# Strassen's sums of weights in the w2 stages: two made by VectorE, two by adding transfers, and five folds in place of six

## The chip, the cores and the metric

The kernel runs on one core of a Trainium2 chip. The metric is the device time of one execution in microseconds (us); lower is better. The core's engines work side by side and wait for one another by semaphores: TensorE (PE: matmuls; PEld is its loading of the stationary operand), VectorE (DVE), ScalarE (ACT), GpSimd (POOL) and SyncE (SP), whose queue here mostly issues transfers. A transfer is issued from an engine's queue and carried out by the core's DMA engines.

## The reference

A decoder trunk of two layers over 256 tokens of width 1024, in float32. Each layer has two half-step feed-forward blocks with a mixer of two branches between them, each followed by a layer norm:

```python
def _swiglu(x, w1, w3, w2):
    return (jax.nn.silu(x @ w1) * (x @ w3)) @ w2

for l in range(DEPTH):                                   # DEPTH = 2
    h = _swiglu(x, ffn_w1[l, 0], ffn_w3[l, 0], ffn_w2[l, 0])
    x = _layernorm(ALPHA * x + 0.5 * h, ln_g[l, 0], ln_b[l, 0])
    h = _mixer(x, l, ...)
    x = _layernorm(ALPHA * x + h, ln_g[l, 1], ln_b[l, 1])
    h = _swiglu(x, ffn_w1[l, 1], ffn_w3[l, 1], ffn_w2[l, 1])
    x = _layernorm(ALPHA * x + 0.5 * h, ln_g[l, 2], ln_b[l, 2])
```

The change concerns the last product of `_swiglu`, with w2: (256 x 2816) times (2816 x 1024). It occurs four times, two layers by two feed-forward blocks; each occurrence is called a w2 stage here.

## The kernel before, in words

Every matmul runs on operands split in two: `hi`, a rounded copy that ScalarE makes, and `lo`, what is left, which VectorE makes by a subtraction (`split`, lines 225 and 227; in `stream`, lines 183 and 185). A product of float32 matrices is then three matmuls: hi by hi, lo by hi, hi by lo. Weights come from HBM in pieces of 128 x 2048 float32 (1 MB). `fetch` (transfer at line 161, on SP's queue) takes a buffer from `raw_pool`, which has four; a buffer is free again when both halves of its piece have been split (or used in a sum). Half a piece, 128 x 1024, is the unit of the splits. The hi and lo pools have eight tiles each.

The hidden activations are in 22 blocks of 128 (k = 0 to 21), the 256 tokens in two blocks (t = 0, 1), the 1024 output columns in two halves (c = 0, 1). `gemm_seven` is a w2 stage. The blocks k = 0 to 7 (a 2 x 2 arrangement of tokens by hidden blocks, times the pieces w11, w12, w21, w22 of four k blocks by one column half) go by Strassen's scheme in Winograd's form: seven products (`product`, line 355, 12 matmuls each) in place of eight. The left sides of four of them are sums of activations, `sums[0]` to `sums[3]`, made beforehand. The right sides of four are sums of weights, of which three build on one another in the buffer r1: w11 + w12, then + w22, then + w21; the fourth is w12 + w22. `gather` (lines 336 to 340) makes such a sum by two adding transfers of 512 KB each, issued from GpSimd's queue (line 339), which add the second piece from HBM onto the buffer.

The products accumulate in PSUM banks, two of them side banks, `bx` and `bz`. Where a product belongs to more than one output block, `ln.fold` (line 567) lets VectorE add or subtract the side bank onto the token tile `xtok`, at 128 x 512. The remaining hidden blocks, k = 8 to 21, are ordinary matmuls (`rows`, line 370). Those of column half 0 are cut into seven pieces of 12 matmuls and stand between the products (`between`), those of column half 1 follow in the end (`held`). Their weights come in the fetches of k = 8, 12, 16 and 20, called R8, R12, R16 and R20 here, one set for each column half.

TensorE's order is the program's; the instructions of the other engines are put in order by a scheduler from priorities that `step()` moves on with each fetch or gather, and from an estimate of when their operands are there. Each engine works through its own queue in that order. Besides the weights the stage has, on the queues of the others: the last two hidden blocks, whose transposes go as transfers on SP's queue (line 202) with copies on GpSimd before and after (lines 198 and 207); the loads of the norm's gain and bias (line 534, GpSimd's queue), in the last stage with a scaling on ScalarE (line 553).

Of the kernel before, what the change touches and what calls it, by code (L numbers as in the profile page):

```python
# [17 lines left out]
ALU = mybir.AluOpType  # L18
# [5 lines left out]
NT = T // P  # L24
# [3 lines left out]
FT = DFF // P  # L28
# [8 lines left out]
CH = 2048  # L37
HC = CH // 2
# [16 lines left out]
def trunk(ctx, tc, x, xT, w13a, w13b, w2, wb, wqk, wu, wg, wgr, wbr, wbrr, wo, gateb, gatebr, sgug, sgub, sguwT, sgubias, lam, diffg,  # L55
          lng, lnb, lngT, lnbT, cosT, sinT, out):
    nc = tc.nc
    V, A, G, PE = nc.vector, nc.scalar, nc.gpsimd, nc.tensor
# [15 lines left out]
    def name(s):  # L74
        serial[0] += 1
        return f"{s}_{serial[0]}"

    def bank():
        return psum.tile([P, 512], F32, tag="main", name=name("bank"))

    def side_bank():
        return psum.tile([P, 512], F32, tag="side", name=name("sbank"))
# [26 lines left out]
    def step():  # L109
        chunk[0] += 1  # L110
        tc.cur_priority = chunk[0] * STEP
# [12 lines left out]
    def beat(w):  # L124

        clock[0] += w
        for task in list(tasks):
            if task[0] <= clock[0]:
                turn(task)
# [18 lines left out]
    def behind(ins):  # L148

        return tc.issue_after(ins) if ins is not None else nullcontext()  # L150

    def fetch(src, width=CH):

        step()
        raw = raw_pool.tile([P, CH], F32, tag="raw", name=name("raw"))
        for g in gate:
            g[0] -= 1
        while len(gate) > 1 and gate[1][0] < 0:
            gate.pop(0)
        with behind(gate[0][1] if gate and gate[0][0] < 0 else None):  # L160
            loaded[0] = nc.sync.dma_start(raw[:, :width], src).ins
        return raw

    def stream(src, width=CH, sub=HC, lent=(), after=(None, None), pool=()):

        raw = fetch(src, width)
        out = []
        first = sooner.pop() if sooner else latest  # L170
        for o in range(0, width, HC):
            eng = G if o // HC in pool else V
            if o // HC in lent:
                hi, lo = ([act.tile([P, 512], F32R, tag="slot", name=name(n)) for _ in range(2)] for n in ("lhi", "llo"))
                at = [(hi[j], lo[j]) for j in range(2)]
            else:
                hi = hi_pool.tile([P, HC], F32R, tag="hi", name=name("whi"))
                lo = lo_pool.tile([P, HC], F32R, tag="lo", name=name("wlo"))
                at = [(hi[:, p : p + sub], lo[:, p : p + sub]) for p in range(0, HC, sub)]
            for p, (h, w) in zip(range(0, HC, sub), at):  # L180
                r = raw[:, o + p : o + p + sub]
                with behind(first[0]):
                    A.activation(h, r, AF.Copy)  # L183
                with behind(after[o // HC] or (first[1] if eng is V else None)):
                    eng.tensor_tensor(out=w, in0=r, in1=h.bitcast(F32), op=ALU.subtract)  # L185
            out.append((hi, lo))
        return out
# [35 lines left out]
    def split(hi, lo, src, eng=V, after=(None, None)):  # L223
        with behind(after[0]):
            a = A.activation(hi, src, AF.Copy).ins  # L225
        with behind(after[1]):
            return a, eng.tensor_tensor(out=lo, in0=src, in1=hi.bitcast(F32), op=ALU.subtract).ins  # L227
# [94 lines left out]
    def gemm_seven(src, xh, xl, sums, ln, done):  # L322

        q = [[bank() for _ in range(NT)] for _ in range(2)]
        bx, bz = side_bank(), side_bank()
        (w11, w21), (w12, w22) = ([s[:, o : o + CH] for o in (0, CH)] for s in src)

        def gather(raw, more):
            step()
            for o in range(0, CH, HC):
                G.dma_start(raw[:, o : o + HC], more[:, o : o + HC], accum_op=ALU.add)  # L339
            return raw  # L340

        def pieces(raw):
            out = []
            for o in range(0, CH, HC):
                hi = hi_pool.tile([P, HC], F32R, tag="hi", name=name("whi"))
                lo = lo_pool.tile([P, HC], F32R, tag="lo", name=name("wlo"))
                split(hi, lo, raw[:, o : o + HC])
                out.append((hi, lo))
            return out

        def product(ps, x, w, start, stop):
            for k in range(4):
                hi, lo = (v[:, k % 2 * 512 : k % 2 * 512 + 512] for v in w[k // 2])
                for n, (y, o) in enumerate(((hi, 0), (lo, 0), (hi, 1))):
                    PE.matmul(ps, x[o](k), y, start=start and k == n == 0, stop=stop and k == 3 and n == 2,  # L355
                              skip_group_check=True)
                beat(0.25)

        def rest(c):
            for k in range(8, FT, 4):  # L360
                nk = min(4, FT - k)
                for j, piece in enumerate(stream(src[c][:, k * 512 : (k + nk) * 512], nk * 512)):
                    yield k + 2 * j, piece

        def rows(t, c, k0, piece, o=0, n=512):
            for j in range(2):
                k = k0 + j
                hi, lo = (w[:, j * 512 + o : j * 512 + o + n] for w in piece)
                for m, (y, x) in enumerate(((hi, xh), (lo, xh), (hi, xl))):
                    PE.matmul(q[c][t][:, :n] if o == 0 else more[:, :n], x(k)[:, t * P : (t + 1) * P], y,  # L370
                              start=k == 8 and m == 0, stop=k == FT - 1 and m == 2, skip_group_check=True)
            beat(n / 1024)

        def block(t, k0):
            return tuple(lambda k, f=f: f(k0 + k)[:, t * P : (t + 1) * P] for f in (xh, xl))

        a11, a12, a22 = block(0, 0), block(0, 4), block(1, 4)
        first = rest(0)

        def between():  # L380
            k, piece = next(first)
            for t in range(NT):
                rows(t, 0, k, piece)

        r1 = fetch(w11)
        product(bx, a11, pieces(r1), True, False)
        ln.fold(0, 0, bx, ALU.add, True)
        between()
        product(bz, sums[0], pieces(gather(r1, w12)), True, False)
        ln.fold(1, 1, bz, ALU.add, True)  # L390
        between()
        product(bx, sums[1], pieces(gather(r1, w22)), False, False)
        ln.fold(0, 1, bx, ALU.subtract, True)
        between()
        product(bz, sums[3], pieces(fetch(w22)), False, True)
        ln.fold(0, 1, bz, ALU.add, False)
        between()
        product(bx, sums[2], pieces(gather(fetch(w12), w22)), False, False)
        ln.fold(1, 1, bx, ALU.subtract, False)
        between()  # L400
        product(q[0][0], a12, pieces(fetch(w21)), False, False)
        between()
        product(bx, a22, pieces(gather(r1, w21)), False, True)
        ln.fold(1, 0, bx, ALU.add, True)
        between()
        for t in range(NT):
            done(t, q[0][t], 0, 512)
        held = list(rest(1))
        cuts = ((0, 512),), (((0, 256), (256, 256)) if ln.last else ((0, 512),))
        for t in range(NT):  # L410
            for o, n in cuts[t]:
                more = bank() if o else None
                for k, piece in held:
                    rows(t, 1, k, piece, o, n)
                done(t, (more if o else q[1][t])[:, :n], 512 + o, n)
# [288 lines left out]
    def ffn(l, f, i, norm, last=False):  # L704
# [75 lines left out]
        def done(t, p, c, n):  # L780
            ln.part(t, c, p, True)
            if c + n == D:
                ln.finish(t, 1.9)

        gemm_seven([w2[l, f, c] for c in range(2)], hh, hl, sums, ln, done)
        return ln.close()

# [389 lines left out]
```

## Time and profile before

| | us |
|---|---|
| median of 3 runs | 1233.73 |
| lowest, highest | 1232.32, 1233.95 |
| the profiled execution | 1235.48 |
| its span in the trace | 1233.70 |

The profiled execution is one run of the program, recorded by the hardware profiler; its mean granted TensorE clock is 0.986 of full speed. The w2 stages begin in it (first product) at 125.10, 547.14, 734.43 and 1157.64 us.

How the rows are read: PE, DVE, ACT, POOL and SP are the engines, with a "q" the engine's queue of issues; L355 is line 355 of the kernel. A row of an engine in order of time has start, duration (both us), line, operation, output and inputs, their sizes, the count of like instructions put together, and in square brackets the idle time before it and what ended that. A row of a group has the count, then minimum, median and maximum in ns. In the waits a row has who waited for whom, us in total, how often, and the longest. In the rows of transfers the last number is the median time from issue to landing. `sbank` is a side bank; `whi`, `wlo` are split weights, `hhi`, `hlo` split activations, `sum` a sum of activations.

### The profile page before, as it was taken

How to read it: one execution, taken by the hardware profiler on the slowest of the kernel's cores; microseconds unless marked ns; L12 is line 12 of the kernel's file. 1: busy time of each engine (PE TensorE's matmuls, PEld its weight loads, DVE VectorE, ACT ScalarE, POOL GpSimd, SP SyncE). 2: the span in 40 equal slices, each digit the busy share in tenths (PEclk: the TensorE clock that was granted, in tenths of full speed). 3: DMA queues.
4: the chain of work that ended last, by engine and by line, in shares of the span. 5: the costliest groups of instructions: out<-in, count | busy, mean ns of one | idle time of the engine just before them, and what ended most of it. 6: DMA issues, size and time to landing. Idle time of an engine off the chain costs nothing.

```text
span 1233.7 us, 16913 instructions
## 1 busy us (share of the span) xinstructions
PE 1206.5 (98%) x5819; PEld 1009.1 (82%) x5819; DVE 948.5 (77%) x1620; ACT 743.8 (60%) x1424; POOL 372.6 (30%) x474
## 2 busy tenths in 40 slices
PE   9999899999999999998999998999999999999898
PEld 8888688888888888886888886888888888888777
DVE  7686689897698977766886866888966988767485
ACT  7474467668865656454655554676787556645461
POOL 1425201256411232540042450003564022334300
PEclk9999999999999999998999998999999999999989
DMA  9959985767765577689776689777676764785891
GB/s 345 321 168 258 238 309 198 259 196 223 234 220 188 173 243 248 169 238 255 254 256 209 192 236 249 265 267 233 214 209 193 260 193 147 276 245 176 209 285 38
DMA packets 128614, 280.36 MB, mean 227 GB/s; under 512 B 88928, under 2 KB 90000, under 8 KB 102416
## 3 DMA queue, kind: packets, MB, share of 16 engines
q1 hardware_dynamic: 119664, 248.80, 61.3%
q0 software_dynamic: 8432, 29.96, 10.7%
q8 instruction: 45, 0.74, 0.2%
q10 hardware_dynamic: 432, 0.52, 0.1%
q14 instruction: 41, 0.34, 0.1%
HBM read 253.30 MB, written 1.05 MB: 206 GB/s over the span
## 4 chain that ended last, share of the span: by engine, by line
PE 88%; DMA 7%; DVE 1%; POOL 1%; ACT 1%; issue 1%; SPq 0%; POOLq 0%; ACTq 0%
PE bank L261 49%; PE bank L273 12%; PE bank L370 11%; PE bank L280 6%; DMA raw<-in_w 5%; PE sbank L355 3%; PE bank L474 2%; DMA planes<-planes 2%; PE sbank L836 1%; PE bank L355 1%; PE sbank L892 1%; PE sbank L1010 1%; DVE wlo L227 0%; POOL raw L339 0%; ACT whi L225 0%
## 5 line engine op out<-in xcount | busy, mean ns | idle before, releaser
L185 DVE TENSOR_TENSOR wlo<-raw,whi 128x512 fp32r<-128x512 f32 (+1 forms) x534 | 475.3, 929 | 66.9 <-ACT whi L183 49.4
L183 ACT ACTIVATE whi<-raw 128x512 fp32r<-128x512 f32 (+1 forms) x538 | 396.2, 783 | 184.8 <-PE bank L261 92.1
L261 PE MATMUL bank<-whi,x 128*128 128x512 f32 x1480 | 460.5, 390 | 0.0
L261 PEld LDWEIGHTS bank<-whi,x 128*128 128x128 f32 x1480 | 277.9, 188 | 57.4
L261 PE MATMUL bank<-wlo,x 128*128 128x512 f32 x740 | 288.0, 389 | 0.0
L198 POOL COPY planes<-planes 128x512 uint16<-128x512 uint16 x80 | 103.9, 1331 | 209.8 <-DVE planes L718 209.8
L261 PEld LDWEIGHTS bank<-wlo,x 128*128 128x128 f32 x740 | 139.0, 188 | 28.5
L273 PE MATMUL bank<-x,whi 128*128 128x512 f32 x640 | 153.3, 391 | 0.0
L273 PEld LDWEIGHTS bank<-x,whi 128*128 128x128 f32 x640 | 118.2, 188 | 23.8
L227 DVE TENSOR_TENSOR wlo<-raw,whi 128x1024 fp32r<-128x1024 f32 (+1 forms) x72 | 77.0, 1102 | 64.3 <-ACT whi L225 50.5
L225 ACT ACTIVATE whi<-raw 128x1024 fp32r<-128x1024 f32 (+1 forms) x72 | 66.1, 956 | 79.7 <-DMA raw<-in_w 72.3
L370 PE MATMUL bank<-whi,hhi 128*128 128x512 f32 (+1 forms) x238 | 91.6, 385 | 0.0
L370 PE MATMUL bank<-wlo,hhi 128*128 128x512 f32 (+1 forms) x238 | 90.9, 382 | 0.0
L370 PE MATMUL bank<-whi,hlo 128*128 128x512 f32 (+1 forms) x238 | 90.4, 380 | 0.0
L718 DVE TENSOR_TENSOR planes<-planes,bank 128x512 f32<-128x512 f32 x40 | 27.3, 683 | 74.6 <-issue 59.9
L717 ACT ACTIVATE planes<-bank 128x512 f32<-128x512 f32 x40 | 23.9, 596 | 99.5 <-PE bank L261 97.1
L280 PEld LDWEIGHTS bank<-x,wlo 128*128 128x128 f32 x640 | 81.4, 191 | 2.9
L280 PE MATMUL bank<-x,wlo 128*128 128x256 f32 x640 | 82.6, 283 | 0.0
L680 POOL COPY nvia<-ntwo 128x256 uint16<-128x256 uint16 x20 | 10.2, 557 | 175.4 <-DMA ntwo<-nvia 157.2
L812 POOL TENSOR_TENSOR swap<-swap,sin_t 128x512 f32<-128x512 f32 x16 | 26.1, 1632 | 100.7 <-DMA swap<-z 47.4
L355 PE MATMUL sbank<-whi,sum 128*128 128x512 f32 x96 | 39.1, 465 | 15.9 <-ACT whi L225 15.9
L370 PEld LDWEIGHTS bank<-whi,hhi 128*128 128x128 f32 x238 | 45.8, 192 | 8.6
(235 smaller groups left out, 1769.1 us busy)
## 6 DMA issues: line engine op xcount, KB each, us to landing
raw<-in_w13b SPq DMA_DIRECT2D x76, 1024.0 KB, 5.8
raw<-in_w SPq DMA_DIRECT2D x40, 1024.0 KB, 6.5
raw<-in_w POOLq DMA_DIRECT2D x32, 512.0 KB, 7.9
raw<-in_wb SPq DMA_DIRECT2D x16, 1024.0 KB, 6.4
raw<-in_wqk SPq DMA_DIRECT2D x16, 1024.0 KB, 5.8
raw<-in_w13a SPq DMA_DIRECT2D x8, 1024.0 KB, 5.1
raw<-in_wgr SPq DMA_DIRECT2D x8, 1024.0 KB, 5.1
raw<-in_wg SPq DMA_DIRECT2D x8, 1024.0 KB, 5.0
```

The costliest lines, as they stand in the source:

```text
L183: A.activation(h, r, AF.Copy)
L185: eng.tensor_tensor(out=w, in0=r, in1=h.bitcast(F32), op=ALU.subtract)
L198: G.tensor_copy(out=planes(out)[:, w], in_=numbers(src)[:, w])
L225: a = A.activation(hi, src, AF.Copy).ins
L227: return a, eng.tensor_tensor(out=lo, in0=src, in1=hi.bitcast(F32), op=ALU.subtract).ins
L261: PE.matmul(ps, xx, w, start=start and n == 0, stop=stop and n == 2)
L273: PE.matmul(b[-1], hi[:, k * P : (k + 1) * P], xc(k), start=k == 0, stop=False)
L280: PE.matmul(b[n][:, :T], lo[:, k * P : (k + 1) * P], xc(k)[:, :T], start=False, stop=k == KT - 1)
L355: PE.matmul(ps, x[o](k), y, start=start and k == n == 0, stop=stop and k == 3 and n == 2, skip_group_check=True)
L370: PE.matmul(q[c][t][:, :n] if o == 0 else more[:, :n], x(k)[:, t * P : (t + 1) * P], y, start=k == 8 and m == 0, stop=k == FT - 1 and m == ...
L718: added[0] = V.tensor_tensor(out=s, in0=s, in1=ps[1], op=ALU.mult).ins
L812: turned_by[0] = G.tensor_tensor(out=s3, in0=s3, in1=s, op=ALU.mult).ins
```

## The change

A second way of adding comes in: `plus`, two VectorE additions of 128 x 1024 of one buffer onto another. w11 + w12 and its sum with w22 are made by it, for which w12 and w22 are fetched into buffers of their own (r2, r3) and stay there: r3 is then the right side of a product itself, and an adding transfer puts w22 onto r2. The last sum, r1 + w21, is made by an adding transfer as before. So a stage has two gathers (2 MB) in place of four and fetches the same four pieces of w11 to w22; each is fetched once.

The order of the last four products is another: the product of `sums[3]` and w22 comes fourth as before, then that of w21, then that of w12 + w22, then the last. The side bank `bz` is now also the accumulation bank of column half 1, second token block (`q[1][0]` in the code's indices: half 1, t = 0). The fourth product stays in it, without a fold; the later matmuls of `rows` for that bank add to it and do not start it afresh. One fold of six goes.

```diff
-        q = [[bank() for _ in range(NT)] for _ in range(2)]
-        bx, bz = side_bank(), side_bank()
+        q = [[bank(), bank()], [side_bank(), bank()]]
+        bx, bz = side_bank(), q[1][0]
...
+        def plus(raw, more):
+            for o in range(0, CH, HC):
+                V.tensor_tensor(out=raw[:, o : o + HC], in0=raw[:, o : o + HC], in1=more[:, o : o + HC], op=ALU.add)
+            return raw
+
...
-                              start=k == 8 and m == 0, stop=k == FT - 1 and m == 2, skip_group_check=True)
+                              start=k == 8 and m == 0 and (c, t) != (1, 0), stop=k == FT - 1 and m == 2, skip_group_check=True)
...
         r1 = fetch(w11)
         product(bx, a11, pieces(r1), True, False)
         ln.fold(0, 0, bx, ALU.add, True)
+        r2 = fetch(w12)
         between()
-        product(bz, sums[0], pieces(gather(r1, w12)), True, False)
+        product(bz, sums[0], pieces(plus(r1, r2)), True, False)
         ln.fold(1, 1, bz, ALU.add, True)
+        r3 = fetch(w22)
         between()
-        product(bx, sums[1], pieces(gather(r1, w22)), False, False)
+        product(bx, sums[1], pieces(plus(r1, r3)), False, False)
         ln.fold(0, 1, bx, ALU.subtract, True)
         between()
-        product(bz, sums[3], pieces(fetch(w22)), False, True)
-        ln.fold(0, 1, bz, ALU.add, False)
-        between()
-        product(bx, sums[2], pieces(gather(fetch(w12), w22)), False, False)
-        ln.fold(1, 1, bx, ALU.subtract, False)
+        product(bz, sums[3], pieces(r3), False, False)
         between()
         product(q[0][0], a12, pieces(fetch(w21)), False, False)
+        between()
+        product(bx, sums[2], pieces(gather(r2, w22)), False, False)
+        ln.fold(1, 1, bx, ALU.subtract, False)
         between()
         product(bx, a22, pieces(gather(r1, w21)), False, True)
         ln.fold(1, 0, bx, ALU.add, True)
```

In the order that results, the queues change too. On SP's queue the fetches of a stage are w11, w12, R8, w22, R12, both transposes of the last hidden block, w21, R16, R20, then the second column half; before they were w11, R8, R12, a transpose, w22, a transpose, w12, R16, w21, R20, then the second column half. The fetch of R12 waits for the buffer of R8, that of w21 for the buffer of R12, that of R16 for the buffer of w22, that of R20 for the buffer of w21.

## The prediction

> **What bounds the kernel now.** First the page, its busy shares:
>
> ```profile
> PE 1206.5 (98%) x5819; PEld 1009.1 (82%) x5819; DVE 948.5 (77%) x1620; ACT 743.8 (60%) x1424; POOL 372.6 (30%) x474
> ```
>
> TensorE is the bound. The change removes no matmul, so it can only give back time in which TensorE waits or runs slowly. Second view: the waits of TensorE, over the whole span. These are its two long groups:
>
> ```profile
> PE sbank L355 <- ACT whi L225: 15.9, 8, 3.7
> PE sbank L355 <- DVE wlo L227: 4.6, 8, 0.8
> ```
>
> Sixteen waits, 20.5 us, all in the product line L355: four in each of the four w2 stages. Third view: TensorE in order of time, picked rows: in the first stage the start (125.10), the waits and the fourth product (149.22); of the others the start and the fourth product, and from the third also two waits.
>
> ```profile
> 125.10 0.40 PE L355 MATMUL sbank<-whi,hhi 128*128 128x512 f32 x1
> ...
> 137.40 0.50 PE L355 MATMUL sbank<-whi,sum 128*128 128x512 f32 x1 [1.23 <-ACT whi L225]
> 138.66 0.50 PE L355 MATMUL sbank<-wlo,sum 128*128 128x512 f32 x1 [0.76 <-DVE wlo L227]
> 142.39 0.50 PE L355 MATMUL sbank<-whi,sum 128*128 128x512 f32 x1 [2.30 <-ACT whi L225]
> 143.65 0.50 PE L355 MATMUL sbank<-wlo,sum 128*128 128x512 f32 x1 [0.76 <-DVE wlo L227]
> 149.22 0.39 PE L355 MATMUL sbank<-whi,sum 128*128 128x512 f32 x1
> ...
> 547.14 0.40 PE L355 MATMUL sbank<-whi,hhi 128*128 128x512 f32 x1
> 573.16 0.39 PE L355 MATMUL sbank<-whi,sum 128*128 128x512 f32 x1
> ...
> 734.43 0.40 PE L355 MATMUL sbank<-whi,hhi 128*128 128x512 f32 x1
> 746.70 0.49 PE L355 MATMUL sbank<-whi,sum 128*128 128x512 f32 x1 [1.20 <-ACT whi L225]
> 747.96 0.53 PE L355 MATMUL sbank<-wlo,sum 128*128 128x512 f32 x1 [0.77 <-DVE wlo L227]
> 749.14 0.63 PE L355 MATMUL sbank<-wlo,sum 128*128 128x512 f32 x1
> 759.72 0.40 PE L355 MATMUL sbank<-whi,sum 128*128 128x512 f32 x1
> ...
> 1157.64 0.40 PE L355 MATMUL sbank<-whi,hhi 128*128 128x512 f32 x1
> 1184.08 0.39 PE L355 MATMUL sbank<-whi,sum 128*128 128x512 f32 x1
> ```
>
> All four gaps of a stage lie in its third product, the one whose weights are w11+w12+w22, two for each half. After them matmuls take 0.63 us in place of 0.39. Why the third product is late is told by the chain in order of time:
>
> ```profile
> 127.87 1.14 DVE wlo L227
> ...
> 129.53 11.67 DMA raw<-in_w
> ...
> 141.28 1.06 ACT whi L225
> ...
> 149.38 2.72 PE sbank L355 x12
> ```
>
> Its columns are start, duration and what. The sum r1 += w22 may start only once the second product's split has read r1 (127.87 + 1.14), and then the adding transfer takes 11.67 us, to 141.20. TensorE wanted its second half near 137.
>
> **What the gaps cost.** A product or a block between two products is 12 matmuls in 2.72 us, 0.2267 us each. From the first product to the fourth there are 72: 16.32 us. The rows give 24.12, 26.02, 25.29 and 26.44 us, so the stages lose 7.80, 9.70, 8.97 and 10.12 us: 36.6 us in all. Of it 20.5 is the gaps; 16.1 is slow matmuls after them. That is the most that the change can bring.
>
> **The third product after the change.** VectorE makes the sum. Its rows of before around that point, and the nearest price for an addition of two 128x1024 float32 operands (line L646):
>
> ```profile
> 130.39 0.67 DVE L567 SCALAR_TENSOR_TENSOR xtok<-xtok,sbank 128x512 f32<-128x512 f32 x1
> 137.38 1.23 DVE L227 TENSOR_TENSOR wlo<-raw,whi 128x1024 fp32r<-128x1024 f32 x1 [6.32 <-ACT whi L225]
> ```
>
> ```profile
> L646 DVE TENSOR_TENSOR xtok<-xtok,bc x20: 1210/1217/1631, 205.6 to 1064.6; 128x1024 f32<-128x1024 f32 x20
> ```
>
> VectorE idled 6.32 us exactly there. Two additions after the fold that ends at 131.06 end at 132.28 and 133.50; ScalarE splits the first half (1.06, as at 141.28) by 133.34; VectorE's two remainders end at 134.73 and 135.96. TensorE asks for the third product at 125.10 + 48 x 0.2267 = 135.98 and for the remainders 0.23 and 1.59 us later. Margin 1.5 us: the four gaps go, all 36.6 us. The additions lie in idle time; a price of 1.63 us takes 0.8 of the margin.
>
> The first sum (w11+w12) has more room: it is wanted for the second product, and VectorE has a gap for its second half:
>
> ```profile
> 115.12 2.86 DVE L185 TENSOR_TENSOR wlo<-raw,whi 128x1024 fp32r<-128x1024 f32 x2
> 122.48 1.22 DVE L227 TENSOR_TENSOR wlo<-raw,whi 128x1024 fp32r<-128x1024 f32 x1 [4.50 <-PE bank L280]
> 144.11 2.35 DVE L185 TENSOR_TENSOR wlo<-raw,whi 128x1024 fp32r<-128x1024 f32 x2
> ```
>
> Cost nothing. A dropped fold (0.67 us) and two adding transfers fewer a stage (2 MB) cost nothing either; the other two have their operands early: w12+w22 some 30 us ahead, r1+w21 from about 136 for a product at 157.7.
>
> **What is late next.** There are four raw buffers, and r1, r2 and r3 now stay pinned, so fetches follow one another through the fourth: w21, which was fetched for the sixth product, is now wanted for the fifth, and its fetch waits until VectorE has split R12 (the column-0 rows from k=12). On SP's queue R16, R20 and the second column stand behind it; both transposes of the last hidden block stand behind R12's fetch.
>
> ```profile
> raw<-in_w SPq DMA_DIRECT2D x40, 1024.0 KB, 6.5
> bc<-in_lng POOLq DMA_DIRECT2D x6, 512.0 KB, 12.1
> bc<-in_gatebr POOLq DMA_DIRECT2D x2, 512.0 KB, 4.5
> planes<-planes SPq DMA_TRANSPOSE x40, 5.9
> ```
>
> After 135.96 VectorE does a fold (0.67) and R12's two remainders (2.35): 138.98, when w21's fetch starts. At 6.5 us it lands at 145.5; split 146.5, remainder 147.8. The fifth product begins at 125.10 + 96 x 0.2267 = 146.86 and wants the remainder at 147.1: gap 0.7 us. Every microsecond of a later landing adds one, and the last adding transfers and R16's fetch are in flight beside it: I take 1.5 us. The clock is added: in the third stage gaps of 1.20 and 0.77 us were enough for 0.63 us matmuls, and in the first stage 7.80 - 5.05 = 2.75 us came on top of its gaps. I take 1.5 more: 3 us in each of three stages, with bounds 0.7 (no slow matmuls) and 5.
>
> The last stage has one more wait: ScalarE's scaling of ln's gain (L553), between the splits of R12's two halves, needs a load from GpSimd's queue.
>
> ```profile
> 1164.03 1.85 POOL L534 DMA_DIRECT2D bc<-in_lng  x1
> 1178.15 1.04 ACT L553 ACTIVATE bc<-bc 128x1024 f32<-128x1024 f32 x1
> ```
>
> With the addition in front, the load is issued near 1165. It lands after 4.5 us (the like-sized gatebr row) to 12.1; I take 7, since the adding transfers that were in its company are gone: 1172. Then scaling, split and remainder (1.04 + 1.04 + 1.2) let w21's fetch go at 1175.3, and its split ends at 1182.9; the fifth product wants it at 1157.64 + 21.76 = 1179.4. A gap of 3.5 to 4, and 2.5 for the clock: 6.5 us, between 2 and 13.
>
> **Two rules against the trace.** The rows at 746.70 to 749.14 show half speed after two gaps of 1.20 and 0.77 us. The Trainium skill ("TensorE: Matmul & The Clock Gate", Part 1) gives the return to half rate after at least one idle window of about 3.4 us; by it gaps of 1.5 us would cost nothing beyond themselves, and the sum would be some 5 to 7 us better. The rows decide against it here.
>
> VectorE's remainders took 2.86 us for two at 115.12, beside GpSimd's copies, and 2.35 at 144.11, away from them: 0.25 us more each.
>
> **The sum.** Gain 36.6, new gaps 3 x 3 + 6.5 = 15.5: 21.1 us less. The profiled execution took 1235.48 us (span 1233.70), 1.75 above the median of 1233.73; the difference is taken from the median: 1212.6 us, I say 1212.5. Its own range: with the small bounds (2.1 + 2) the gain is 32.5, 1201; with the large ones (15 + 13) it is 8.6, 1225.
>
> **Rivals.**
> *No new wait at all.* w21 lands within 5.5 us and the last stage's load is early: 36.6 us, 1197; for it, 2 MB less traffic; against it, the three pinned buffers. 1197 to 1201.
>
> *VectorE's queue stands still behind others.* Between the second addition and its remainder VectorE makes remainders of hidden planes, which wait for GpSimd's joins of the two transposes, now queued on SP behind R12's fetch. At rows' durations these are through by about 130 (fetch 119.2, transposes issued by 122, 5.9 us, copies), 3.5 us in time. Beside the copies VectorE could also be held for a whole one:
>
> ```profile
> 115.38 1.59 POOL L207 COPY planes<-planes 128x512 uint16<-128x512 uint16 x1 [1.71 <-DMA planes<-planes]
> ```
>
> Two such holds are 3.2 us: less the margin, 1.7 us of gap at the third product, and 3.2 more at the fifth; 4.9 a stage, 19.6 in all: 1232. With one hold, 1226. The row of 0.25 us speaks against it. The Trainium skill ("SBUF — State Buffer", the section on the two separate sides) says this: a VectorE operation with two SBUF inputs and a GpSimd operation that reads SBUF exclude each other for the whole instruction. By it this rival's holds would be the normal case wherever the two meet.
>
> *Slower: w21 arrives late.* The fifth product takes over from the third. Landing 12 us after its fetch, as the chain's transfer (11.67) and ln's gain (12.1) did, its gap is 6.2 us and 2.75 of clock, 9 us in three stages and 12 in the last: 39 us, 1236; at 14 us, 1244. It is slower from a landing of about 11.4 us. For it: in that stretch w21, R16 and the adding transfers run together. Against: SP's own fetches have a median of 6.5 us.
>
> **How the numbers follow.** Forecast 0.60 (1201 to 1225), no new wait 0.08, VectorE held 0.15 (1226 to 1235), w21 late 0.17 (1236 to 1246). About 0.2% (2.5 us) is what a measurement of this kernel can tell from no change. Faster: 0.60 + 0.08 + 0.09 of the third = 0.77; same: 0.05, the rest of the third but for 0.01; slower 0.18. The range leaves out some 0.05 below 1200 and 0.15 above 1237.
>
> **What would show it.** Right: TensorE's waits on L355 at the third product are gone in all four stages; the largest remaining ones stand at the fifth product, with w21's transfer behind them, 1 to 2 us each and 3 to 4 in the last stage; the first product to the fourth takes 16.3 to 17 us. Wrong: gaps at the third product behind VectorE's or GpSimd's operations; w21 landing over 10 us after its issue; gaps at R16's block or in the second column; remainders of 128x1024 well over 1.25 us in the stages.

## The result

The changed kernel took 1226.78 us (median; 1224.23 to 1228.29), the kernel before 1233.84 us: ratio 0.9942, 95% interval 0.9922 to 0.9962. It is faster by 0.6% (0.4 to 0.8), 7.1 us, where 21 were forecast. The gain is a third of the forecast one, and the time lies just above the forecast's own range (1201 to 1225), in that of the rival in which VectorE's queue stands still (1226 to 1235).

The profiled execution took 1224.23 us, the fastest of four; its span is 1222.50 us against 1233.70 before. The page of the changed kernel, and TensorE's waits in it (who waited for whom, us in total, times, longest); `product` is now line 360, `rows` 375, the additions 344, the fold 573:

```profile
PE 1200.6 (98%) x5819; PEld 1005.2 (82%) x5819; DVE 964.6 (79%) x1632; ACT 745.0 (61%) x1424; POOL 365.1 (30%) x458
```

```profile
PE bank L360 <- ACT whi L225: 5.4, 3, 2.2
PE sbank L360 <- ACT whi L225: 4.2, 1, 4.2
PE bank L360 <- DVE wlo L227: 3.0, 4, 0.8
PE sbank L360 <- DVE wlo L227: 1.8, 3, 0.8
PE sbank L360 <- DVE xtok L573: 1.7, 2, 1.1
```

Where there were 20.5 us of waits on the products there are 16.1. "bank" is the fifth product, "sbank" the others: at third products one wait of 4.2 us is left and three of 0.8 or less behind VectorE's remainders. The two waits for `xtok` (1.7 us) stand at the seventh product: it writes the side bank `bx`, which the fold of the sixth must have read, and in the new order only one block lies between the two. TensorE in order of time, picked rows of the four stages (first and seventh product, and the longer waits between):

```profile
125.19 0.40 PE L360 MATMUL sbank<-whi,hhi 128*128 128x512 f32 x1
...
149.18 0.50 PE L360 MATMUL bank<-whi,hhi 128*128 128x512 f32 x1 [1.76 <-ACT whi L225]
150.44 0.50 PE L360 MATMUL bank<-wlo,hhi 128*128 128x512 f32 x1 [0.76 <-DVE wlo L227]
...
154.09 0.63 PE L360 MATMUL bank<-whi,hlo 128*128 128x512 f32 x1
...
162.82 0.39 PE L360 MATMUL sbank<-whi,hhi 128*128 128x512 f32 x1
...
544.38 0.40 PE L360 MATMUL sbank<-whi,hhi 128*128 128x512 f32 x1
...
559.61 0.80 PE L360 MATMUL sbank<-whi,sum 128*128 128x512 f32 x1 [4.16 <-ACT whi L225]
...
586.72 0.47 PE L360 MATMUL sbank<-whi,hhi 128*128 128x512 f32 x1 [1.08 <-DVE xtok L573]
...
731.75 0.40 PE L360 MATMUL sbank<-whi,hhi 128*128 128x512 f32 x1
...
756.31 0.50 PE L360 MATMUL bank<-whi,hhi 128*128 128x512 f32 x1 [2.23 <-ACT whi L225]
...
769.13 0.47 PE L360 MATMUL sbank<-whi,hhi 128*128 128x512 f32 x1 [0.62 <-DVE xtok L573]
...
1150.84 0.40 PE L360 MATMUL sbank<-whi,hhi 128*128 128x512 f32 x1
...
1163.25 0.50 PE L360 MATMUL sbank<-wlo,sum 128*128 128x512 f32 x1 [0.75 <-DVE wlo L227]
...
1176.37 0.50 PE L360 MATMUL bank<-whi,hhi 128*128 128x512 f32 x1 [1.42 <-ACT whi L225]
...
1190.04 0.39 PE L360 MATMUL sbank<-whi,hhi 128*128 128x512 f32 x1
```

From the first to the seventh product there are 144 matmuls, 32.64 us at 0.2267 us each. The stages take 37.63, 42.34, 37.38 and 39.20, so 5.0, 9.7, 4.7 and 6.6 us are lost: 26.0 in all, against 36.6 before. The difference, 10.6 us, is the difference of the spans (11.2) but for 0.6. In the first and third stage the third product is in time and the loss stands at the fifth, as forecast. In the second stage the third product still comes 4.3 us late, and its block and the next lose 7.2 us together; in the fourth they lose 2.2.

What holds the third product of the second stage is read from the queues, each in order of time: SP, GpSimd, ScalarE, VectorE.

```profile
537.44 0.33 SPq L161 DMA_DIRECT2D raw<-in_w  x1
537.82 5.70 SPq L202 DMA_TRANSPOSE planes<-planes  x2
```

```profile
539.26 0.86 POOL L339 DMA_DIRECT2D raw<-in_w  x1 [1.38 <-DVE raw L344]
544.79 1.62 POOL L207 COPY planes<-planes 128x512 uint16<-128x512 uint16 x2 [4.66 <-DMA planes<-planes]
553.96 1.43 POOL L207 COPY planes<-planes 128x512 uint16<-128x512 uint16 x2 [7.55 <-DMA planes<-planes]
```

```profile
555.43 0.42 ACT L743 ACTIVATE hhi<-planes 128x256 fp32r<-128x256 f32 x1 [8.57 <-POOL planes L207]
555.75 0.40 ACT L225 ACTIVATE hhi<-silu 128x256 fp32r<-128x256 f32 x1
```

```profile
556.18 0.42 DVE L227 TENSOR_TENSOR hlo<-silu,hhi 128x256 fp32r<-128x256 f32 x1 [7.69 <-ACT hhi L225]
...
556.59 0.68 DVE L573 SCALAR_TENSOR_TENSOR xtok<-xtok,sbank 128x512 f32<-128x512 f32 x1
557.18 2.35 DVE L344 TENSOR_TENSOR raw<-raw,raw 128x1024 f32<-128x1024 f32 x2
```

R12's fetch goes at 537.44, both transposes of the last hidden block right behind it, and at 539.26 the second half of the adding transfer onto r2. GpSimd joins the second transpose only at 553.96, 9.6 us after the stage's first product; in the first stage it is 4.0 us. ScalarE's hidden planes wait for the join; the next row in ScalarE's queue (555.75) makes what VectorE waits for, so VectorE stands 7.69 us, and behind that stand the fold and the two additions. The fold ends at 557.27, 12.9 us after the stage's first product, where the prediction had 6.0 (131.06 less 125.10). The transfers of that stretch, issue to landing:

```profile
raw<-in_w POOLq DMA_DIRECT2D x1, 512.0 KB, 14.3
bc<-in_lng POOLq DMA_DIRECT2D x1, 512.0 KB, 3.6
planes<-planes SPq DMA_TRANSPOSE x2, 10.8
```

The second transpose took 14.7 us and the adding transfer 14.3; they end together. The prediction had 5.9 us for a transpose.

### The profile page after: what moved, and what is told of

Read it like the earlier page. It is cut to its first block, busy times and chain, and to the rows that moved or that the text cites. A ratio compares the mean times of both kernels' runs of the same rounds, so it can differ in the third digit from the quotient of the medians.

```text
span 1222.5 us, 16873 instructions
## 1 busy us (share of the span) xinstructions
PE 1200.6 (98%) x5819; PEld 1005.2 (82%) x5819; DVE 964.6 (79%) x1632; ACT 745.0 (61%) x1424; POOL 365.1 (30%) x458
## 5 line engine op out<-in xcount | busy, mean ns | idle before, releaser
L198 POOL COPY planes<-planes 128x512 uint16<-128x512 uint16 x80 | 110.1, 1404 | 211.6 <-DVE planes L724 208.9
L375 PE MATMUL bank<-whi,hhi 128*128 128x512 f32 (+1 forms) x182 | 68.6, 377 | 0.0
L375 PE MATMUL bank<-wlo,hhi 128*128 128x512 f32 (+1 forms) x182 | 68.3, 375 | 0.0
L375 PE MATMUL bank<-whi,hlo 128*128 128x512 f32 (+1 forms) x182 | 67.9, 373 | 0.0
L207 POOL COPY planes<-planes 128x512 uint16<-128x512 uint16 x48 | 38.5, 841 | 45.3 <-DMA planes<-planes 45.2
L281 ACT ACTIVATE r<-bank 128x256 f32<-128x256 f32 x96 | 34.7, 371 | 21.7 <-PE bank L280 21.7
```

The costliest lines, as they stand in the source:

```text
L198: G.tensor_copy(out=planes(out)[:, w], in_=numbers(src)[:, w])
L207: eng.tensor_copy(out=numbers(out)[:, w], in_=planes(src)[:, w])
L281: emptied[0] = A.activation(r[:, s], b[n][:, T:], AF.Copy, scale=scale).ins
```

## The experiments

All times are medians beside runs of the kernel before on the same chip (1233.99 us for the first four, 1233.67 for the last four). "Lost" is what the four stages' first to seventh products take beyond 32.64 us each, in the profiled execution.

**The changed kernel again.** No edit.

> The changed kernel once more, nothing edited, to see which of its gaps come back in every execution. If the third product's gap of the second stage (4.2 us in the first profile, behind transposes that took 14.7 us to land) belongs to that stage, it stands there again; if it is a matter of chance in the transfers, it is smaller or stands in another stage, and the time moves by up to 7 us from run to run. Expected time 1224 to 1229 us; the gaps at the fifth product (1.4 to 2.2 us) are there in either case.

Measured: 1229.92 us, ratio 0.997 (0.9955 to 0.9984). Lost 4.8, 10.4, 5.5, 8.4 us. This is a gain of 4 us, less than the 7 of the first measurement. The third product of the second stage was late again, by 4.6 us, and this time also that of the fourth, by 3.1; the second transposes landed after 8.9, 15.0, 7.8 and 16.2 us. So the late landings stand in the same two stages as before, and that in the fourth was 2.8 us later still.

**Products five and six changed back.**

```diff
-        product(q[0][0], a12, pieces(fetch(w21)), False, False)
-        between()
         product(bx, sums[2], pieces(gather(r2, w22)), False, False)
         ln.fold(1, 1, bx, ALU.subtract, False)
+        between()
+        product(q[0][0], a12, pieces(fetch(w21)), False, False)
```

> Products five and six change places, as they stood before: the sum w12+w22 fifth, w21 sixth. Theory A: the fifth product waits because w21's fetch may start only when VectorE has split R12, 139 to 140 us in the first stage, and lands 8 us later; a product later (5.44 us) it is in time. Then the gaps at the fifth product go in all four stages, 4.5 + 1.2 + 3.5 + 4.4 us with the slow matmuls after them: about 13 us less than the changed kernel, 1211 to 1216. Rival: VectorE has no time left in that stretch, the splits of R16 and of the sum come late instead, and a gap of the same size stands at the fifth or sixth product: 1223 to 1229.

Measured: 1217.55 us, ratio 0.9855 (0.9831 to 0.9879). Theory A holds: no gap at the fifth product in any stage. The time is still above theory A's range, because 18.5 us are lost at third products, against 10 in the changed kernel. Lost 1.0, 11.2, 7.4, 1.0 us, all but 2 at the third product and after it in the second and third stage; in the second TensorE's row shows

```profile
559.11 0.79 PE L360 MATMUL sbank<-whi,sum 128*128 128x512 f32 x1 [7.74 <-ACT whi L225]
```

and the second transposes landed after 18.3 and 14.8 us. The adding transfer beside the first of them took 18.4 us.

**Transposes ahead of R12's fetch.** In the steps of a hidden block's transposes, for the last block only:

```diff
-            yield from transposed(s, p[:, 0], p[:, 1], lead, wait - lead, 0.6, G, to)
+            d = 2.5 if n == NB - 1 else 0
+            yield from transposed(s, p[:, 0], p[:, 1], lead, wait - lead - d, 0.6 + d, G, to)
```

> The two transposes of the last hidden block are issued ahead of the fetch of R12 instead of behind it, nothing else. Theory B: in the second and fourth stage the transposes land after 14.7 and 13.4 us because R12's megabyte goes ahead of them; VectorE stands at the remainders of that block, and the sum w11+w12+w22 behind it is late. Then the transposes land in under 9 us in all stages, the gap at the third product goes (7.2 us in the second stage, 1.9 in the fourth): 1217 to 1220. Rival: it is the adding transfer issued beside them that delays them (its own landing was 14.3 and 13.1 us there); then the landing and the gap stay, 1224 to 1229. The gaps at the fifth product stay in both.

Measured: 1205.69 us (1205.25 to 1206.69), ratio 0.9771 (0.9756 to 0.9786). Far more than expected: lost 1.0, 2.1, 2.2, 1.4 us. SP's queue in the first stage, in order of time:

```profile
111.28 0.33 SPq L161 DMA_DIRECT2D raw<-in_w  x1
111.65 8.38 SPq L202 DMA_TRANSPOSE planes<-planes  x2
120.55 20.10 SPq L161 DMA_DIRECT2D raw<-in_w  x3
```

The first transpose now goes at 111.65, before it had stood behind R12's fetch until 118.62; the second at 118.8, alone. The eight land after 2.7 to 8.0 us. The third product is in time everywhere. That the gaps at the fifth product ("bank") nearly went as well was not expected; TensorE's waits:

```profile
PE sbank L360 <- DVE xtok L573: 2.6, 4, 1.0
PE bank L360 <- DVE wlo L227: 1.7, 3, 0.8
...
PE bank L360 <- ACT whi L225: 0.3, 1, 0.3
```

VectorE's first fold began at 129.60 us here, at 131.83 in the changed kernel; w21's fetch followed as much earlier and landed after 6.7 us instead of 7.7, so that its split began 3.2 us earlier, and the gaps at that product had been 1.76 and 0.76. Most of what is left are waits of the seventh product for the fold of the sixth (2.6 us).

**Both edits.**

> The two edits together: products five and six changed back, transposes ahead of R12's fetch. If theories A and B hold, both kinds of gaps go and all 36.6 us but a few: 1203 to 1208 us. If only A holds 1211 to 1216, if only B 1217 to 1220.

Measured: 1198.78 us (1198.36 to 1198.94), ratio 0.9712 (0.9697 to 0.9727), better than expected. Lost 0.2 us in the four stages together; no wait on a product is left, not at the seventh either, since the sixth no longer uses `bx`.

```profile
PE 1191.6 (100%) x5819; PEld 1002.9 (84%) x5819; DVE 963.8 (81%) x1632; ACT 745.0 (62%) x1424; POOL 364.0 (30%) x458
```

This version beats both kernels: 35 us under the one before, where 36.6 was the most to be had.

**Without the adding transfers onto r2.**

```diff
-        product(bx, sums[2], pieces(gather(r2, w22)), False, False)
+        product(bx, sums[2], pieces(r2), False, False)
```

> The changed kernel without the adding transfers onto r2: its product takes w12 where w12 + w22 belongs, so one of the seven products is of other numbers. It tells what makes the transposes of the last hidden block land late (8 to 16 us). If it is the adding transfer issued within 2 us of them, which landed in 13 to 14 us in the same stages, they land in under 9 us in all stages and the third product has no gap: with the gaps at the fifth product left, 1212 to 1218. If it is R12's fetch ahead of them and their being issued as a pair, landing times and gaps stay: 1222 to 1230.

This kernel leaves w22 out of the sum w12 + w22. Measured: 1211.52 us, ratio 0.9829 (0.9815 to 0.9842). The transposes are issued as in the changed kernel, as a pair behind R12's fetch (first stage: 118.7 and 120.4). Their landing, as minimum, median and maximum, in the second stage of the changed kernel and of this one:

```profile
L202 SPq DMA_TRANSPOSE planes<-planes x2: 1231/2802/4372, 537.8 to 539.1; - x2
...
DMA to landing us min/median/max: 6.8/10.8/14.7
```

```profile
L202 SPq DMA_TRANSPOSE planes<-planes x2: 1232/2595/3958, 537.1 to 538.4; - x2
...
DMA to landing us min/median/max: 6.5/7.0/7.6
```

In all four stages they land in 6.1 to 7.6 us, and no third product waits. What is lost, 4.2, 4.5, 4.5 and 3.2 us, stands at the fifth product and after it. So it is the adding transfers onto r2, the second of which goes beside them, that make the transposes late, not R12's megabyte nor their being a pair: theory B had the right cure and the wrong cause.

**Five folds alone**, in the kernel before (`bz` as accumulation bank `q[1][0]`, that is column half 1 and the first token block, t = 0, where "The change" says the second; no fold after the fourth product; adding transfers kept).

```diff
-        q = [[bank() for _ in range(NT)] for _ in range(2)]
-        bx, bz = side_bank(), side_bank()
+        q = [[bank(), bank()], [side_bank(), bank()]]
+        bx, bz = side_bank(), q[1][0]
...
-        product(bz, sums[3], pieces(fetch(w22)), False, True)
-        ln.fold(0, 1, bz, ALU.add, False)
+        product(bz, sums[3], pieces(fetch(w22)), False, False)
```

> The kernel before, with the side bank bz made the accumulation bank of the second column half and the fold after the fourth product left away; the sums of weights stay adding transfers. The fold (0.68 us of VectorE, four times) lies where VectorE waits for weights, so it costs nothing: within 0.2% of the kernel before, 1231 to 1236. Rival: a fold less brings forward w22's or R16's split, and a part of the gain is the fold's: 1228 or less.

Measured: 1232.91 us, ratio 0.9989 (0.9977 to 1.0002). No difference that can be told; lost 36.5 us, as before.

**Only the second sum by VectorE**, in the kernel before, with `plus` as in the changed one.

```diff
...
+        r3 = fetch(w22)
         between()
-        product(bx, sums[1], pieces(gather(r1, w22)), False, False)
+        product(bx, sums[1], pieces(plus(r1, r3)), False, False)
...
-        product(bz, sums[3], pieces(fetch(w22)), False, True)
+        product(bz, sums[3], pieces(r3), False, True)
```

> The kernel before, with one of its four sums made by VectorE: r1 += w22, for which w22 is fetched early and kept until its own product; order of the products and six folds as before. If that one sum is what the 36.6 us hang on, the third product's gap goes in all stages unless the transposes, which here too are issued as a pair behind R12's fetch but without R12 waiting for a buffer, land late: 1198 to 1206. If the pair behind the fetch is enough to make them late, gaps of 3 to 8 us at the third product come in two stages of four: 1212 to 1225.

Measured: 1209.09 us, ratio 0.979 (0.9775 to 0.9805), with a wide spread (1204.77 to 1218.52; the profiled one is the slowest). Lost in it 5.6, 1.4, 1.5, 8.4 us: in the second and third stage the transposes landed within 6.7 us, in the first and fourth they took up to 18.1 and 16.5. The issues stand alike in all four, an adding transfer of the first sum 1.3 us behind the first transpose; in the first stage these adding transfers took 14.1 and 14.8 us. The transposes stand behind R12's fetch here too (112.1 in the first stage), but not as the pair that was expected: they go at 112.5 and 119.4. This one sum is the bulk of the possible gain (25 of 36.6 us), and the disturbance is the same.

**First sum by an adding transfer again**, in the version with both edits.

```diff
-        product(bz, sums[0], pieces(plus(r1, r2)), True, False)
+        product(bz, sums[0], pieces(gather(r1, w12)), True, False)
```

> The version with both edits (products five and six changed back, transposes ahead of R12's fetch), but the first sum, w11 + w12, made by an adding transfer again as in the kernel before; w12 is still fetched for r2. If only the second sum has to be VectorE's, as the gaps of the kernel before say, the time is that of the version with both edits, 1197 to 1201. If the 1 MB of adding traffic comes in the way of the transposes or of R12, the second or third product gets gaps: 1203 to 1215.

Measured: 1219.69 us (1219.39 to 1220.1), ratio 0.989 (0.9876 to 0.9903): 21 us worse than with both edits. In the first stage three adding transfers go at 111.5 to 113.2 and one at 115.4, the transposes at 112.0 and 118.9; the transposes land after 11 to 18 us in all four stages, the adding transfers after 8.8 to 13.1 us in the first. ScalarE and VectorE stand for w11 + w12, and what VectorE has behind it is late, the last hidden activations among it, so that TensorE's gap is in the first block between products. VectorE in the first stage, then TensorE's waits:

```profile
126.89 1.23 DVE L227 TENSOR_TENSOR wlo<-raw,whi 128x1024 fp32r<-128x1024 f32 x1 [8.53 <-ACT whi L225]
```

```profile
PE bank L375 <- DVE silu L283: 9.6, 4, 3.1
```

So VectorE's first sum matters too, though no product of the kernel before waited for it: with it no adding transfer for which something waits soon runs beside the transposes.

## Why the prediction was right or wrong

**What is to be had** (36.6 us): right. The span less what is lost is 1197.1 us before, 1196.5 for the changed kernel, 1196.9 with the transposes moved, 1196.9 with both edits. And 1198.78 is a run of it.

**The third product by VectorE's additions:** right where its operands and VectorE's queue were free. In the first stage the additions took 2.35 us for two, as priced, and the product came in time, though with less margin: the fold ended at 132.5, not 131.06, since VectorE waited 2.10 us behind ScalarE's hidden planes. From the first product to the fourth it took 16.6, 23.6, 16.7 and 18.5 us, where 16.3 to 17 was the sign of being right: it came in two stages of four.

**What is late next, w21:** right in place and about right in size. Without the adding transfers all four stages lose 16.4 us, against 15.5 in the sum, and that kernel's time is 1211.5 against the 1212.5 forecast. That the sum fits so closely is partly luck, for its terms were off both ways: 4.2 to 4.5 where 3 was taken, 3.2 in the last stage where 6.5 was. The wait of the seventh product for the fold of the sixth was not in the sum at all (2.2 us in that kernel). The load of ln's gain, for which 7 us were taken, landed after 3.7.

**The step that failed** is the landing of the transposes: "through by about 130 (fetch 119.2, transposes issued by 122, 5.9 us, copies), 3.5 us in time". The issue was right (118.6, 120.4), the 5.9 us were not: 8.6, 14.7, 8.7 and 13.4 us for the second one. 5.9 was the median of transposes that had no adding transfer issued within 2 us of them. In place of "the four gaps go, all 36.6 us", it cost 7.2 us in the second stage and 2.2 in the fourth, and in the second profile 7.4 and 6.4: 26.0 us are lost in all, 10.5 more than the sum's 15.5, and 9.4 of them stand here. The rival named the right queue (VectorE standing at the planes behind the joins, 1226 to 1235 with 0.15), but priced it by holds beside GpSimd's copies, which was not what happened; that the measured time lies in its range is partly luck.

**The port rule** weighed there: an addition that began beside GpSimd's copies took 1.62 us, away from them 1.18.

```profile
115.67 3.03 POOL L198 COPY planes<-planes 128x512 uint16<-128x512 uint16 x2 [0.66 <-ACT whi L183]
```

```profile
118.14 1.62 DVE L344 TENSOR_TENSOR raw<-raw,raw 128x1024 f32<-128x1024 f32 x1
...
132.42 2.35 DVE L344 TENSOR_TENSOR raw<-raw,raw 128x1024 f32<-128x1024 f32 x2
```

The copies ended at 118.70, so 0.56 us of the second was left when the addition began, and the addition took 0.45 us more, alike in all four stages. So the small extra does not speak against the section of the Trainium skill ("SBUF — State Buffer", on the two separate sides), as the prediction took it to do: VectorE lost about what was left of the copy. What did not come is the rival's price, a whole copy of 1.59 us each time.

**The slower rival** (w21 landing after 11 us or more): did not come; 7.2 to 8.1 us in the four stages.

**The profiled execution against the median:** 1.75 us were taken as the offset. The changed kernel's profile is 2.6 below its median, which is most of what lies between 11.2 us by the spans and 7.1 by the medians. The likely reason is that how late the transposes land changes from execution to execution; the two profiles show it, the other executions have none.

## What to carry to other kernels

A landing time from a group's median holds only for the company that the group had: when a change moves a transfer, price it by rows in which the same neighbours were in flight, and where there are none, put the whole length of the neighbour on the upper bound; and look which of the two is issued first, since late or not went with that here. Before pricing an operation that waits, look what stands behind it on its in-order engine: here a late transpose of 256 KB, which TensorE did not need yet, held VectorE's sums, which it did. When a change shows a third of its gain, a small move of the disturbed transfer is worth trying before the change is judged: the same change with its transposes moved gains 28 us and with two products changed back 35.

## What the runs showed of the hardware

Transposes by DMA and adding transfers issued within about 1.5 us of each other can delay one another, and then end together: 14.7 and 14.3 us, 18.3 and 18.4, where the same pair of transposes without the adding transfer took 6.1 to 7.6. Which stage it hits goes with the order of the two issues. In the second stage of the changed kernel the second transpose goes first, at 539.14, and the adding transfer 0.12 us behind it. In the first stage the adding transfer goes first, 0.35 us ahead (GpSimd's row, then the two transposes of that stage, the second at 120.4, and their landing):

```profile
120.07 0.87 POOL L339 DMA_DIRECT2D raw<-in_w  x1 [1.38 <-DVE raw L344]
```

```profile
L202 SPq DMA_TRANSPOSE planes<-planes x2: 1280/2540/3801, 118.6 to 120.4; - x2
...
DMA to landing us min/median/max: 6.9/7.8/8.6
```

So it is in all twelve stages of the three profiles with this pair of issues (the changed kernel, the same again, products five and six changed back). In six the adding transfer was issued 0.06 to 0.12 us behind the second transpose, which took 13.4 to 18.3 us; in six it was issued 0.15 to 0.90 us ahead, and the transpose took 7.8 to 9.0. In the run with the products changed back the order is the other way round in the third and fourth stage, and the late transpose moved from the fourth to the third with it. No run here changes the order alone, and with the adding transfer 1.3 us behind (only the second sum by VectorE) it went both ways. In the kernel before and with the transposes moved, where over 2 us lay between them, no transpose of these blocks took more than 8.0, but for one of 10.9 (both edits), which ended together with an adding transfer issued 2.5 us behind it: 2 us apart is no safe distance.

In the second stage of the changed kernel the end of it is a tail in which few DMA engines work. Its windows (bounds and length, then busy time of PE, PEld, DVE, ACT and POOL, clock, DMA share, GB/s) show the tail in the second stage, then a stretch of the first stage with adding transfers in flight, and one right after it, in which the fetches of w21 and R16 move (the last packets of an adding transfer, landed at 147.72, are among them):

```profile
549.00:553.00 4.00, 4.00 (x19) 3.32 (x18) 0.00 (x0) 0.00 (x0) 0.00 (x0) 1.00 0.29 29
136.50:143.50 7.00, 7.00 (x31) 5.56 (x31) 7.00 (x9) 3.65 (x5) 1.77 (x2) 1.00 0.80 133
144.00:148.00 4.00, 3.42 (x16) 2.49 (x14) 0.13 (x1) 0.00 (x0) 0.00 (x0) 1.00 1.01 415
```

29 GB/s at a share of 0.29 in the tail; 133 GB/s at 0.80 with the adding transfers against 415 at 1.01 with mostly fetches. Which DMA engines the tail sits on, and why the order of the issues should matter, stays open. And gaps of 1.76 and 0.76 us were enough to bring matmuls of 0.63 us (the rows at 149.18 to 154.09; the granted clock was 0.50 from 152 to 154), as in the kernel before. Each gap, and the two together, are under the idle window of about 3.4 us in the Trainium skill ("TensorE: Matmul & The Clock Gate", Part 1).
